# The fourth mixer of a two-block transformer kernel: TensorE's order written by hand, the index path first, two heads' queries at a time

## The chip, the cores and the metric

The kernel is one program on one core of a Trainium2 chip. A core has five engines that run side by side, each through its own queue of instructions: TensorE (PE in the profile: matmuls and transposes), VectorE (DVE), ScalarE (ACT), GpSimd (POOL) and SyncE (SP), which here issues the transfers. The metric is the time of one execution on the device in microseconds (us); less is better.

## The reference

Two transformer blocks run one after the other on 256 tokens of width 1024, all in 32-bit floats. The second block puts 16 meta tokens ahead of the 256 and has two layers: one with differential attention, one (the fourth mixer of the program) with an indexed latent attention, `_dsa_attention`. Each layer has two feed-forward networks around its mixer.

```python
def _dsa_attention(h, pos, cid, w_in, latent_norm, w_uq, q_norm, w_uv, rel_bias, k_sel):
    c_q, c_kv, k_idx, w_idx = jnp.split(h @ w_in, ...)        # 256, 256, 64 and 8 columns
    c_q = _rms_norm(c_q, latent_norm[0])
    c_kv = _rms_norm(c_kv, latent_norm[1])
    q_abs, q_idx = jnp.split(c_q @ w_uq, [B_HEADS * B_KV_RANK], axis=-1)   # 16 heads of 256; 8 index heads of 64
    q_abs = _rms_norm(q_abs.reshape(bsz, t, B_HEADS, B_KV_RANK), q_norm)
    k_idx = _rms_norm(k_idx)
    ...
        act = jax.nn.relu(jnp.einsum("bqhd,bsd->bqhs", qi, k_idx) * IDX_DIM ** -0.5)
        score = jnp.einsum("bqh,bqhs->bqs", wi, act)
        _, sel = lax.top_k(score, k_sel)                       # 64 keys of each query
        kv = gather(c_kv, sel)
        logits = jnp.einsum("bqhr,bqkr->bqhk", qa, kv) * B_KV_RANK ** -0.5 + bias
        p = jax.nn.softmax(jnp.where(valid, logits, NEG_INF), axis=-1)
        o_lat = jnp.einsum("bqhk,bqkr->bqhr", p, kv)
        o = jnp.einsum("bqhr,hrd->bqhd", o_lat, w_uv)
```

## The kernel before

**Precision.** A product of two 32-bit operands is made of three matmuls: each operand is split in a high and a low part, and `mm3` (L212 to L214) adds high·high, high·low and low·high. A weight arrives by DMA as `raw`, ScalarE casts its high part (`wh`, L187), and VectorE subtracts to get the low part (`wl`, L189). For the pieces in the table `ON_POOL` (L75) GpSimd does that subtraction. A piece has 1024 columns, or 512.

**Streaming.** `stream_plan` lists all weight pieces in the order of use, by name: `bw` (down-projection to the query latent), `bwi` (index key), `bw2` (key and value latent), `bwx` (index weights), `uqi` (index queries), `uq` (queries, two heads in a piece), `uv` (values, four heads in a piece). `take` hands out a piece; `ahead` starts the next loads, four pieces ahead.

**What sets the order.** Each engine runs its instructions in a fixed order that a tile scheduler chooses when the program is built, from the dependences and its own estimate of durations; the text of `dsa_mix` is only one input to it. A PSUM bank is a tile too: there are two tagged `mm`, two `s`, one `b`, one `n` and two `o`. A matmul that starts a new use of a bank stands behind the last read of its old use.

**The fourth mixer, `dsa_mix` (L991).** Rows are 272 tokens. From the normed input come the query latent (L1011 scales by the row's norm, L1023 and L225 split it into `cqh` and `cql`), the index key `ki` (L1036 to L1042), the key and value latent (L1047 to L1052: `ckg` for scores, `ckvh` and `ckvl` for values) and the index weights (L1060). Each of the 8 index heads has a score of all keys (matmuls L220), a relu on ScalarE (`rl`, L1084) and a weighted sum on VectorE (`sc`, L1089 for the first head, L1091 for the others; 16 instructions, since each head has two pieces of 272 and 144 columns). `top_rounds` then finds the 64 largest in eight rounds; a round is two MAX8 and two MATCH_REPLACE (L1104, L1105), all on VectorE and one behind another through `wk`. L1214 and L1215 make the mask `msk` of it.

Beside this, `prep(h)` projects one head's queries into an `mm` bank (12 matmuls), squares them on ScalarE (L1148), makes a norm of 128x2 numbers (`rsq`: Ln and Exp on ScalarE, L247 to L252; one refinement, on GpSimd for the first two heads, L255 to L257 with L258 on VectorE, on VectorE for the others, L261 to L263), scales the bank into `qx` (ScalarE at L1152 for heads 0 and 1, VectorE at L1154 for the others), transposes it into bank `n` (L1158) and copies it to `q` (L1160, ScalarE). The norm's result is `qst`.

`attend(h)` takes the scores of head h (L1177, bank `s`), adds bias and mask (L1179; GpSimd has added `msk` to the bias `nb` at L1165), takes the exponential (L1181), the reciprocal (L1183), scales (L1185, GpSimd), transposes the probabilities into bank `b` (`probs_t`, L977 to L980) and, for each two heads, multiplies by the values `v`, which `values(g)` makes for four heads at a time (18 matmuls, copies L1121 and L1124). Queries are made `LAG` = 4 heads ahead of `attend`.

Of the kernel before, what the change touches and what calls it, by code (L numbers as in the profile page):

```python
# [74 lines left out]
ON_POOL = {("uq", 0, 0), ("uq", 1, 0), ("bw2", 0, 0), ("bw2", 0, 1)}  # L75
# [4 lines left out]
def stream_plan():  # L80
# [32 lines left out]
    put("bwi", 1, 1024)  # L113
    put("bw2", 1, 2048)
    put("bwx", 1, 64)
# [5 lines left out]
    put("uq", 2, 1024, 3)  # L121
    put("uv", 1, 512, 2)
    put("uq", 2, 1024, 5)
    put("uv", 1, 512, 3)
    put("uq", 1, 1024, 7)
    wo(3)
    ffn(5)
    return plan


class Net:
    def __init__(self, ctx, tc, a, out):
# [75 lines left out]
    def mm3(self, out, w, x, first, last, chk=False):  # L208
        mm = self.nc.tensor.matmul
# [6 lines left out]
    def both(self, jobs, start, stop):  # L216


        for out, w, x in jobs[::-1]:
            self.nc.tensor.matmul(out, w, x, start=start, stop=stop, skip_group_check=True)  # L220
# [44 lines left out]
    def sumsq(self, src, cols, on_pool=()):  # L265
# [18 lines left out]
        if n > 1:  # L284
            nc.tensor.matmul(b[:, :cols], self.ones, acc[:, :cols], start=True, stop=False)
        nc.tensor.matmul(b[:, :cols], self.ones, sq[:, :cols], start=n == 1, stop=True)
# [204 lines left out]
    def cols_of(self, r_row, dst):  # L491

        b = self.bank("o")
        for tt in range(2):
            self.nc.tensor.transpose(b[:, tt * P : (tt + 1) * P], r_row[:, tt * P : (tt + 1) * P], self.ident)
        self.nc.vector.tensor_copy(dst, b[:, : 2 * P].rearrange("p (a b) -> p a b", a=2)[:, :, 0])

    def mem_pair(self, qm, mk, mv, p, y, pt, nb=2):
# [7 lines left out]
        for s in ss:  # L506
# [40 lines left out]
    def block1_mix0(self, Xr):  # L547
# [4 lines left out]
        with ExitStack() as ctx:  # L552
# [4 lines left out]
            for k in range(KD):  # L557
# [3 lines left out]
                nc.tensor.matmul(ss[:, :S], self.ones, sq, start=k == 0, stop=k == KD - 1)  # L561
# [55 lines left out]
    def block1_mix1(self, Xr):  # L617
        nc = self.nc
        self.banks(mm=2, z=4, o=2)
        with ExitStack() as ctx:  # L620
# [17 lines left out]
            def pair(p, q):  # L638
# [4 lines left out]
                for z in zs:  # L643
# [9 lines left out]
                    mm = nc.tensor.matmul  # L653
# [57 lines left out]
    def rel_table(self, pool):  # L711
# [9 lines left out]
        for lo, hi in ((0, 512), (512, RELW)):  # L721
            b = self.bank("o")
            nc.tensor.matmul(b[:16, : hi - lo], nrb, oh[:, lo:hi], start=True, stop=True)
# [22 lines left out]
    def boundary_ffn(self, X):  # L746

        nc = self.nc
        with ExitStack() as ctx:
# [19 lines left out]
            for b, sq, cols in zip(ss, sums, (S, T)):  # L769
                nc.tensor.matmul(b[:, :cols], self.ones, sq[:, :cols], start=True, stop=True)  # L770
# [14 lines left out]
    def diff_mix(self, X, Xf):  # L785
# [3 lines left out]
        with ExitStack() as ctx:  # L789
# [10 lines left out]
            nc.tensor.matmul(lb[:, :2], self.ones[:64], pr, start=True, stop=True)  # L800
# [27 lines left out]
            def prep(h):  # L828
# [16 lines left out]
                for i in range(2):  # L845
                    ss = self.bank("n")
                    nc.tensor.matmul(ss[:, :T], self.blk, sq[:, i], start=True, stop=True)  # L847
# [12 lines left out]
            def values(h):  # L860
# [7 lines left out]
                nc.tensor.transpose(b[:, 0], vx[:, 48 : 48 + P], self.ident)  # L868
                nc.tensor.transpose(b[:, 1], vx[:, 48 + P :], self.ident)
                nc.tensor.transpose(b[:48, 2], vx[:, :48], self.ident)  # L870
# [9 lines left out]
            def attend(h):  # L880
# [34 lines left out]
                for i, (oc, pc, v) in enumerate(self.v_parts(vr, vm[:, h], vq)):  # L915
                    nc.tensor.matmul(os[0][:, e * S + oc.start : e * S + oc.stop], v, pr[:, pc],  # L916
# [6 lines left out]
            def sub_norm(o, yh, yl, n, w, tag, tmp=(pt, "o", 2 * S)):  # L923
# [5 lines left out]
                nc.tensor.matmul(ss[:, :cols], self.ones, sq, start=True, stop=True)  # L929
# [4 lines left out]
            def meta(h0, h1):  # L934
# [14 lines left out]
                for h in range(n):  # L949
                    nc.tensor.transpose(b[:NM, h * NM : (h + 1) * NM], v[:, 0, h], self.ident[:NM, :NM])  # L950
# [3 lines left out]
                for h in range(n):  # L954
                    c = slice(h * NM, (h + 1) * NM)
                    nc.tensor.matmul(o[:, c], vm[:NM, h0 + h], ph[:, c], start=True, stop=True)
# [16 lines left out]
    def probs_t(self, L, pt, b, bufs=None):  # L973


        tr = self.nc.tensor.transpose
# [14 lines left out]
    def dsa_mix(self, X, Xr, Xf):  # L991
        nc, a = self.nc, self.a
        NH, LAG, NB = 16, 4, 3
        self.banks(mm=2, s=2, b=1, n=1, o=2)
        with ExitStack() as ctx:
            p1 = self.pool("dsas", 1, ctx=ctx)
            stage = ctx.enter_context(ExitStack())
# [31 lines left out]
            self.ahead()  # L1029
            xs, r = latent(bq, NM, S, pa)  # L1030
            for k in range(2):
                scaled(cq, k, 0, xs[k], self.g("cq", k), r, S)
            (bi,) = self.dense("bwi", xp, T, m_n=1)
            self.ahead()
# [4 lines left out]
            ssk = self.bank("n")  # L1039
            nc.tensor.matmul(ssk[:, :T], self.blk, kq, start=True, stop=True)  # L1040
            self.rsq(kq, ssk[:, :T], 64)
            nc.vector.scalar_tensor_tensor(ki, ki, 0.125, kq, ALU.mult, ALU.mult)  # L1042
            bk = self.dense("bw2", xp, T)
# [333 lines left out]
```

## Time and profile before

| | |
|---|---|
| median of 3 runs | 1721.84 us (1720.2 to 1722.18) |
| the profiled execution, its own time | 1716.95 us |
| span of its instructions | 1715.2 us |
| PE busy | 1678.1 us, 98% of the span |
| DVE busy | 1103.9 us, 64% |
| ACT busy | 895.9 us, 52% |
| POOL busy | 375.6 us, 22% |
| the fourth mixer, from the first `bwi` matmul to the start of its output projection | about 1380 to 1510 us of the span |

The profile comes from one execution. Every instruction has its start and duration on its engine; where an engine was idle, the trace says for how long and whose result ended it. The clock that the throttle granted to TensorE is given by stretch, 1.00 for the higher of its levels and 0.50 for half of that. All times of rows count from the start of the span; the execution's own time is 1.75 us longer than its span.

### The profile page before, as it was taken

Reading aid. Unit: us, or ns where it says so; the run is one execution under the profiler, and the core shown is the slowest. Engines: PE = TensorE matmul, PEld = TensorE weight load, DVE = VectorE, ACT = ScalarE, POOL = GpSimd, SP = SyncE. Lnnn points to the kernel's source line nnn. Section 1 sums busy time; section 2 is a strip of 40 time slices with the busy share of each in tenths; the row PEclk is TensorE's granted clock in tenths of the full one; section 3 lists DMA queues with packets and bytes.
Section 4 is the critical chain, followed back from the end, with each engine's and each line's share of the span. In section 5 each row is a group of like instructions: output and inputs, shape, how many; then the busy total and the mean of one; then the engine's idle time right before and its main releaser. Section 6 shows DMA issues by size and latency. Waiting matters only on the chain.

```text
span 1715.2 us, 32923 instructions
## 1 busy us (share of the span) xinstructions
PE 1678.1 (98%) x13474; PEld 1633.1 (95%) x13474; DVE 1103.9 (64%) x1808; ACT 895.9 (52%) x1554; POOL 375.6 (22%) x402
## 2 busy tenths in 40 slices
PE   7999999999999999999999999999999989999999
PEld 7999999998899999999988999999999977899999
DVE  7767666565766566655788766556665576666652
ACT  6545445476544555444566544445444457754441
POOL 3013220011322013211421222211221224432210
PEclk9999999999999999999999999999999999999999
DMA  8456655432555545445642454554454333335551
GB/s 282 167 195 225 229 185 185 172 124 99 174 195 179 191 172 174 177 176 180 193 127 89 147 174 174 174 182 171 177 177 174 124 126 126 124 136 186 183 192 69
DMA packets 59495, 287.56 MB, mean 168 GB/s; under 512 B 12064, under 2 KB 22816, under 8 KB 27472
## 3 DMA queue, kind: packets, MB, share of 16 engines
q1 hardware_dynamic: 58512, 284.80, 47.6%
q8 instruction: 106, 1.74, 0.4%
q10 hardware_dynamic: 832, 0.66, 0.1%
q14 instruction: 45, 0.37, 0.1%
HBM read 284.34 MB, written 5.53 MB: 169 GB/s over the span
## 4 chain that ended last, share of the span: by engine, by line
PE 92%; DVE 4%; ACT 1%; issue 1%; DMA 1%; POOL 0%; SPq 0%; ACTq 0%; DVEq 0%; POOLq 0%
PE mm L212 21%; PE mm L213 21%; PE mm L214 21%; PE z L214 8%; PE z L212 8%; PE z L213 8%; DVE wl L189 1%; PE s L1177 1%; PE o L220 1%; PE z L220 1%; DVE xl L229 1%; PE o L916 1%; DMA X<-in_xT_dram 1%; PE s L220 1%; PE n L847 0%
## 5 line engine op out<-in xcount | busy, mean ns | idle before, releaser
L187 ACT CAST wh<-raw 128x1024 fp32r<-128x1024 f32 (+1 forms) x521 | 540.5, 1040 | 634.3 <-PE mm L213 418.2
L189 DVE TENSOR_TENSOR wl<-raw,wh 128x1024 fp32r<-128x1024 f32 (+1 forms) x513 | 631.7, 1233 | 315.3 <-ACT wh L187 312.6
L212 PE MATMUL mm<-xh,wh 128*128 128x256 f32 (+2 forms) x1768 | 510.0, 289 | 5.4 <-DVE X L388 2.2
L213 PE MATMUL mm<-xl,wh 128*128 128x256 f32 (+2 forms) x1768 | 506.1, 286 | 4.0 <-DVE xl L229 3.7
L214 PE MATMUL mm<-xh,wl 128*128 128x256 f32 (+2 forms) x1768 | 506.3, 286 | 0.0
L212 PEld LDWEIGHTS mm<-xh,wh 128*128 128x128 f32 (+1 forms) x1768 | 333.4, 189 | 11.7 <-issue 2.8
L213 PEld LDWEIGHTS mm<-xl,wh 128*128 128x128 f32 (+1 forms) x1768 | 332.8, 188 | 8.0 <-DVE xl L229 4.9
L214 PEld LDWEIGHTS mm<-xh,wl 128*128 128x128 f32 (+1 forms) x1768 | 333.6, 189 | 1.2 <-issue 0.6
L214 PE MATMUL z<-xh,wl 128*128 128x256 f32 (+1 forms) x1088 | 311.0, 286 | 0.0
L213 PE MATMUL z<-xl,wh 128*128 128x256 f32 (+1 forms) x1088 | 309.9, 285 | 0.0
L212 PE MATMUL z<-xh,wh 128*128 128x256 f32 (+1 forms) x1088 | 309.6, 285 | 0.0
L212 PE MATMUL mm<-gh,wh 128*128 128x256 f32 (+1 forms) x1056 | 300.5, 285 | 0.0
L214 PE MATMUL mm<-gh,wl 128*128 128x256 f32 (+1 forms) x1056 | 299.5, 284 | 0.0
L213 PE MATMUL mm<-gl,wh 128*128 128x256 f32 (+1 forms) x1056 | 299.5, 284 | 0.0
L344 POOL TENSOR_TENSOR es<-es,r 128x256 f32<-128x256 f32 (+1 forms) x110 | 157.1, 1428 | 483.8 <-ACT es L343 483.8
L214 PEld LDWEIGHTS z<-xh,wl 128*128 128x128 f32 x1088 | 205.5, 189 | 0.2
L212 PEld LDWEIGHTS z<-xh,wh 128*128 128x128 f32 x1088 | 205.2, 189 | 0.0
L213 PEld LDWEIGHTS z<-xl,wh 128*128 128x128 f32 x1088 | 204.8, 188 | 0.0
L213 PEld LDWEIGHTS mm<-gl,wh 128*128 128x128 f32 x1056 | 199.2, 189 | 0.0
L214 PEld LDWEIGHTS mm<-gh,wl 128*128 128x128 f32 x1056 | 198.5, 188 | 0.0
L212 PEld LDWEIGHTS mm<-gh,wh 128*128 128x128 f32 x1056 | 198.4, 188 | 0.0
L345 DVE TENSOR_TENSOR ea<-z,es 128x256 f32<-128x256 f32 (+1 forms) x132 | 57.1, 433 | 96.1 <-PE z L214 52.1
(362 smaller groups left out, 1793.3 us busy)
## 6 DMA issues: line engine op xcount, KB each, us to landing
raw<-in_gu_dram SPq DMA_DIRECT2D x132, 1024.0 KB, 4.8
raw<-in_wd_dram SPq DMA_DIRECT2D x66, 1024.0 KB, 4.8
raw<-in_wo_dram SPq DMA_DIRECT2D x13, 1024.0 KB, 4.8
raw<-in_aw_dram SPq DMA_DIRECT2D x12, 1024.0 KB, 4.8
raw<-in_a_in_dram SPq DMA_DIRECT2D x9, 1024.0 KB, 5.3
nb<-scr SPq DMA_DIRECT2D x32, 136.0 KB, 2.4
scr<-relrow SPq DMA_DIRECT2D x16, 271.5 KB, 5.2
raw<-in_mkv_dram SPq DMA_DIRECT2D x4, 1024.0 KB, 4.8
```

The source lines that it names most:

```text
L187: self.nc.scalar.copy(h[:, :c], t[:, x : x + c])
L189: eng.tensor_tensor(l[:, :c], t[:, x : x + c], h[:, :c].bitcast(F32), ALU.subtract)
L212: mm(out, wh, xh, start=first, stop=False, skip_group_check=chk)
L213: mm(out, wh, xl, start=False, stop=False, skip_group_check=chk)
L214: mm(out, wl, xh, start=False, stop=last, skip_group_check=chk)
L220: self.nc.tensor.matmul(out, w, x, start=start, stop=stop, skip_group_check=True)
L229: self.nc.vector.scalar_tensor_tensor(l, src, col, h.bitcast(F32), ALU.mult, ALU.subtract)
L344: nc.gpsimd.tensor_tensor(s, s, r, ALU.mult)
L345: nc.vector.tensor_tensor(a, B[:, :cols], s, ALU.mult)
L916: nc.tensor.matmul(os[0][:, e * S + oc.start : e * S + oc.stop], v, pr[:, pc], start=e == 0 and i == 0, stop=e == 1 and i == 3, skip_group ...
L1177: nc.tensor.matmul(s[:, c], q[:, k, qc], ckg[:, k, k0 : k0 + n], start=k == 0, stop=k == 1)
```

## The change

The arithmetic of the reference and the matmuls that do it stay. What changes is the order, the banks and who does the small work of the fourth mixer:

- **Order by hand.** `Ordered` wraps TensorE's calls as `self.pe`. From `bwi` on until `turn(5)` has been written, every TensorE instruction of these lines is kept in the order of the text. Instructions of `attend` are written later and stay free for the scheduler.
- **Index first.** `bwi` goes to a bank `s`, `bwx` comes ahead of `bw2`, and the norm of the key and value latent moves from ahead of the index scores to between the rounds. `bw2`'s second half is cut in two around the third pair of index heads.
- **Two heads at a time.** `prep` becomes `project(h)`, which projects two heads into both `mm` banks and makes one norm of 128x4 numbers, on VectorE alone, and `turn(h)`, which transposes one head. ScalarE scales heads 0 to 5, VectorE the others. `LAG` becomes 6, and `values(1)` is written ahead of the last rounds.
- **Low parts on GpSimd.** `ON_POOL` gains `uq` pieces 2 and 3 and `uv` piece 0.

```diff
-ON_POOL = {("uq", 0, 0), ("uq", 1, 0), ("bw2", 0, 0), ("bw2", 0, 1)}
+ON_POOL = {("uq", j, 0) for j in range(4)} | {("bw2", 0, 0), ("bw2", 0, 1), ("uv", 0, 0)}
...
     put("bwi", 1, 1024)
+    put("bwx", 1, 64)
     put("bw2", 1, 2048)
-    put("bwx", 1, 64)
...
-        NH, LAG, NB = 16, 4, 3
+        NH, LAG, NB = 16, 6, 3
...
+            self.in_order = True
+            (bi,) = self.dense("bwi", xp, T, m_n=1, ps=("s",))
...
+            def project(h):
+
+                wq = self.take("uq", 2)
+                st = self.t(pq, [P, 2, 2], "qst")
+                b3s = []
+                for e in range(2):
+                    b3 = self.bank().rearrange("p (a b) -> p a b", a=2)
...
+                    qx = qxs[h + e] = self.t(pq, [P, 2, S], "qx")
+                    for tt in range(2):
+                        nc.scalar.activation(qx[:, tt], b3[:, tt], AF.Square, accum_out=st[:, e, tt : tt + 1])
+                    b3s.append(b3)
+                self.ahead()
+                v = st.rearrange("p a b -> p (a b)")
+                self.rsq(v, v, 256, tmp=(pq, "q", 4))
...
+            index_scores(0)
+            index_scores(2)
+            bk[1] = self.bank("n")
+            self.over_k(bk[1][:, :T], wk2[1], xks, range(KD), 0, 4)
+            index_scores(4)
+            self.over_k(bk[1][:, :T], wk2[1], xks, range(KD), 4, KD)
+            self.ahead()
+            index_scores(6)
...
+            project(0)
+            top_rounds(0, 1)
+            xs, r = latent(bk, 0, T, p1)
+            top_rounds(1, 2)
...
+            turn(0)
+            turn(1)
+            project(2)
             top_rounds(2, 4)
-            prep(2)
+            values(0)
+            turn(2)
+            turn(3)
+            project(4)
             top_rounds(4, 6)
-            prep(3)
-            values(0)
+            values(1)
+            turn(4)
+            turn(5)
+            self.in_order = False
             top_rounds(6, 8)
```

The orders below are those of the built programs: line, operation, result and operands, with a number for each tile. In the changed program all lines of the fourth mixer are 17 to 50 higher, and every TensorE instruction stands at L140.

**TensorE, first heads, before.** `s` are scores of a head, `mm_16634` a part of `values(0)` (its factors `ckvh`, `ckvl` and the `uv` weights), `b` the transposed probabilities of head 0, `n` the transposed queries of head 3.

```order
L1177 MATMUL s_16891<-ckg_16064,q_16573 128x144 x2
L1177 MATMUL s_16891<-ckg_16064,q_16573 128x272 x2
L212 MATMUL mm_16634<-wh_16316,ckvh_16062 128x256
L213 MATMUL mm_16634<-wl_16317,ckvh_16062 128x256
L214 MATMUL mm_16634<-wh_16316,ckvl_16063 128x256
L212 MATMUL mm_16634<-wh_16316,ckvh_16062 128x256
L213 MATMUL mm_16634<-wl_16317,ckvh_16062 128x256
L214 MATMUL mm_16634<-wh_16316,ckvl_16063 128x256
L977 MATMUL b_16737<-ident,L_2353_16438 128x128
L1158 MATMUL n_16619<-ident,qx_16606 128x128 x4
```

The same place after: scores of heads 0 and 1, the four transposes of head 0's probabilities, then `values(0)`.

```order
L140 MATMUL s_16827<-ckg_16067,q_16512 128x144 x2
L140 MATMUL s_16827<-ckg_16067,q_16512 128x272 x2
L140 MATMUL s_16860<-ckg_16067,q_16519 128x144 x2
L140 MATMUL s_16860<-ckg_16067,q_16519 128x272 x2
L140 MATMUL b_16839<-ident,L_2367_16492 128x128 x4
L140 MATMUL mm_16583<-wh_16314,ckvh_16065 128x256
L140 MATMUL mm_16583<-wl_16315,ckvh_16065 128x256
L140 MATMUL mm_16583<-wh_16314,ckvl_16066 128x256
```

Ahead of the first transposed probabilities stood three heads' scores, twelve matmuls of `values(0)` and the queries of heads 0 to 3, the first three of them transposed; now two heads' scores, no value, and the queries of heads 0 to 3, the first two of them transposed. `values(0)`, the turns of heads 2 and 3 and the third score stand behind.

**VectorE, from the first round to the first norm's result, before.** `m` are the eight largest, `qst_16456` is the norm of head 0, which the scaling at L1152 waits for.

```order
L1104 MAX m_2362_16477<-sc_16366 128x8
L1104 MAX m_2363_16480<-sc_16366 128x8
L1105 MATCH_REPLACE wk_16425<-m_2362_16477,sc_16366 128x272
L1105 MATCH_REPLACE wk_16425<-m_2363_16480,sc_16366 128x144
L1104 MAX m_2364_16483<-wk_16425 128x8
L1104 MAX m_2365_16486<-wk_16425 128x8
L1105 MATCH_REPLACE wk_16425<-m_2364_16483,wk_16425 128x272
L1105 MATCH_REPLACE wk_16425<-m_2365_16486,wk_16425 128x144
L258 SCALAR_TENSOR_TENSOR qst_16456<-qnr_16459,qnr_2359_16460 128x2
```

After, behind the second round: `qnr` and `qst_16407` are the norm of heads 0 and 1, `nr` and `latr` that of the key and value latent, `wl_16664` the low part of `uq` piece 5.

```order
L208 TENSOR_TENSOR wl_16664<-raw_16661,wh_16663 128x1024
L1121 MAX m_2383_16571<-wk_16267 128x8
L1121 MAX m_2384_16574<-wk_16267 128x8
L280 SCALAR_TENSOR_TENSOR qnr_2351_16447<-qst_16407,qnr_16446 128x4
L280 SCALAR_TENSOR_TENSOR nr_2364_16476<-o_16471,nr_16475 128x272
L1122 MATCH_REPLACE wk_16267<-m_2383_16571,wk_16267 128x272
L1122 MATCH_REPLACE wk_16267<-m_2384_16574,wk_16267 128x144
L281 SCALAR_TENSOR_TENSOR qnr_2351_16447<-qnr_2351_16447,qnr_16446 128x4
L281 SCALAR_TENSOR_TENSOR nr_2364_16476<-nr_2364_16476,nr_16475 128x272
L1121 MAX m_2385_16577<-wk_16267 128x8
L1121 MAX m_2386_16580<-wk_16267 128x8
L282 SCALAR_TENSOR_TENSOR qst_16407<-qnr_2351_16447,qnr_16446 128x4
```

The norm's result came behind two rounds; it comes behind two rounds, a low part, a third round and the two MAX of a fourth, with two steps of the latent's norm between.

**GpSimd, the same stretch, before.** `wl_16250` and `wl_16256` are the low parts of `uq` pieces 0 and 1.

```order
L189 TENSOR_TENSOR wl_16250<-raw_16247,wh_16249 128x1024
L189 TENSOR_TENSOR wl_16256<-raw_16253,wh_16255 128x1024
L1047 TENSOR_TENSOR lat_2307_16259<-lat_2307_16259,latr_2314_16270 128x272
L1047 TENSOR_TENSOR lat_2309_16261<-lat_2309_16261,latr_2314_16270 128x272
L1052 COPY ckvh_16062<-ckvh_16062 128x2x32
```

After, with `uv` piece 0 (`wl_16315`) and `uq` pieces 2 and 3 (`wl_16321`, `wl_16557`):

```order
L208 TENSOR_TENSOR wl_16218<-raw_16215,wh_16217 128x1024
L208 TENSOR_TENSOR wl_16309<-raw_16264,wh_16308 128x1024
L208 TENSOR_TENSOR wl_16315<-raw_16312,wh_16314 128x512
L208 TENSOR_TENSOR wl_16321<-raw_16318,wh_16320 128x1024
L208 TENSOR_TENSOR wl_16557<-raw_16554,wh_16556 128x1024
L1244 MEMSET L_2367_16492 128x16
L1244 MEMSET L_2368_16493 128x16
L1246 TENSOR_TENSOR lat_2355_16463<-lat_2355_16463,latr_2362_16474 128x272
```

Three subtractions come ahead of the scaling of the key and value latent, and that scaling itself has moved behind the first rounds.

## Rows read from the trace of the kernel before

**Rows 1.** The page: busy time, share of the span and instructions of each engine
```profile
PE 1678.1 (98%) x13474; PEld 1633.1 (95%) x13474; DVE 1103.9 (64%) x1808; ACT 895.9 (52%) x1554; POOL 375.6 (22%) x402
```

**Rows 2.** 2-us stretches: length, busy PE, PEld, DVE, ACT, POOL, clock, DMA share, GB/s
```profile
1404.00:1406.00 2.00, 0.94 (x9) 0.57 (x5) 2.00 (x6) 1.41 (x4) 0.11 (x1) 1.00 0.88 270
1406.00:1408.00 2.00, 0.00 (x0) 0.00 (x0) 2.00 (x8) 2.00 (x9) 0.00 (x0) 1.00 0.63 183
1408.00:1410.00 2.00, 0.00 (x0) 0.00 (x0) 2.00 (x10) 0.72 (x5) 0.59 (x3) 0.55 0.51 131
1410.00:1412.00 2.00, 1.00 (x5) 0.82 (x5) 2.00 (x12) 1.30 (x5) 0.16 (x1) 0.50 0.00 0
1412.00:1414.00 2.00, 2.00 (x12) 2.00 (x11) 2.00 (x13) 1.22 (x3) 0.43 (x3) 0.50 0.00 0
1414.00:1416.00 2.00, 2.00 (x11) 1.89 (x11) 2.00 (x10) 1.25 (x6) 0.00 (x0) 0.74 0.00 0
```

**Rows 3.** PE in order of time: start, duration, line, result, [idle before, whose result ended it]
```profile
1396.94 0.49 PE L220 MATMUL s<-ki,qi 64*128 64x272 f32 x1
...
1411.00 1.27 PE L1158 MATMUL n<-ident,qx 128*128 128x128 f32 x4 [6.06 <-ACT qx L1152]
...
1421.88 1.67 PE L1177 MATMUL s<-ckg,q 128*128 128x144 f32 x8 [0.97 <-ACT q L1160]
...
1425.38 0.33 PE L977 MATMUL b<-ident,L 128*128 128x128 f32 x1 [1.12 <-POOL L L1185]
...
1427.51 0.27 PE L979 MATMUL b<-ident,L 128*128 128x128 f32 x1
1427.62 0.27 PE L980 MATMUL b<-ident,L 128*128 128x128 f32 x1
...
1429.13 1.57 PE L1177 MATMUL s<-ckg,q 128*128 128x144 f32 x8
1430.33 0.48 PE L212 MATMUL mm<-wh,ckvh 128*128 128x256 f32 x1
1430.65 0.28 PE L213 MATMUL mm<-wl,ckvh 128*128 128x256 f32 x1
1430.77 0.28 PE L214 MATMUL mm<-wh,ckvl 128*128 128x256 f32 x1
...
1432.30 0.39 PE L212 MATMUL mm<-wh,ckvh 128*128 128x256 f32 x1 [0.45 <-ACT v L1121]
```

**Rows 4.** DVE in order of time, as rows 3
```profile
1398.51 0.91 DVE L1089 TENSOR_SCALAR sc<-rl,wc 128x272 f32<-128x272 f32 x1 [0.89 <-ACT rl L1084]
...
1400.78 1.21 DVE L189 TENSOR_TENSOR wl<-raw,wh 128x1024 fp32r<-128x1024 f32 x1
...
1407.80 0.66 DVE L1104 MAX8 m<-sc 128x8 f32<-128x272 f32 x2
...
1419.51 0.37 DVE L1215 TENSOR_SCALAR msk<-msk 128x432 f32<-128x432 f32 x1
...
1421.58 1.84 DVE L189 TENSOR_TENSOR wl<-raw,wh 128x1024 fp32r<-128x1024 f32 x1
```

**Rows 5.** POOL in order of time, as rows 3
```profile
1365.47 2.40 POOL L189 TENSOR_TENSOR wl<-raw,wh 128x1024 fp32r<-128x1024 f32 x1 [4.07 <-ACT wh L187]
...
1397.77 1.49 POOL L1047 TENSOR_TENSOR lat<-lat,latr 128x272 f32<-128x272 f32 x2 [12.40 <-DVE latr L263]
...
1419.96 4.98 POOL L1165 TENSOR_TENSOR nb<-nb,msk 128x144 f32<-128x144 f32 x7 [7.37 <-DVE msk L1215]
```

**Rows 6.** Line L229: count, least/median/greatest duration in ns, first and last start
```profile
L229 DVE SCALAR_TENSOR_TENSOR xl<-X,gains,xh x2: 495/1232/1970, 1366.2 to 1375.6; 128x272 fp32r<-128x272 f32 x2
L229 DVE SCALAR_TENSOR_TENSOR ckvl<-lat,gains,ckvh x2: 486/486/486, 1401.9 to 1402.3; 128x272 fp32r<-128x272 f32 x2
```

**Rows 7.** The same columns as rows 2: nine stretches of 8 us, 1438 to 1510, summed
```profile
sum 72.00, PE 70.37 PEld 62.32 DVE 46.09 ACT 52.90 POOL 26.01; mean PE 7.82 PEld 6.92 DVE 5.12 ACT 5.88 POOL 2.89
```

**Rows 8.** A short idle time of PE near 1522, as rows 3
```profile
1523.33 0.39 PE L213 MATMUL mm<-xl,wh 128*128 128x256 f32 x1 [1.91 <-DVE xl L229]
```

**Rows 9.** The same columns as rows 2: two stretches around rows 8
```profile
1522.00:1524.00 2.00, 0.67 (x5) 0.67 (x6) 2.00 (x4) 0.35 (x1) 1.79 (x2) 1.00 0.38 70
1524.00:1526.00 2.00, 2.00 (x11) 1.81 (x10) 2.00 (x4) 0.47 (x2) 0.00 (x0) 0.57 0.89 360
```

More of the change, by code (lines that the diff above doesn't have):

```diff
@@ L219, in both @@
         for out, w, x in jobs[::-1]:
-            self.nc.tensor.matmul(out, w, x, start=start, stop=stop, skip_group_check=True)
+            self.pe.matmul(out, w, x, start=start, stop=stop, skip_group_check=True)
     def split_act(self, h, l, src):
@@ L722, in rel_table @@
             b = self.bank("o")
-            nc.tensor.matmul(b[:16, : hi - lo], nrb, oh[:, lo:hi], start=True, stop=True)
+            self.pe.matmul(b[:16, : hi - lo], nrb, oh[:, lo:hi], start=True, stop=True)
             nc.vector.tensor_copy(t[:, lo:hi], b[:16, : hi - lo])
@@ L769, in boundary_ffn @@
             for b, sq, cols in zip(ss, sums, (S, T)):
-                nc.tensor.matmul(b[:, :cols], self.ones, sq[:, :cols], start=True, stop=True)
+                self.pe.matmul(b[:, :cols], self.ones, sq[:, :cols], start=True, stop=True)
             r1 = self.t(p, [P, S], "r1")
@@ L799, in diff_mix @@
             lb = self.bank("n")
-            nc.tensor.matmul(lb[:, :2], self.ones[:64], pr, start=True, stop=True)
+            self.pe.matmul(lb[:, :2], self.ones[:64], pr, start=True, stop=True)
             le = p1.tile([P, 2], F32, name="lame")
@@ L928, in sub_norm @@
                 ss = self.bank(tag)
-                nc.tensor.matmul(ss[:, :cols], self.ones, sq, start=True, stop=True)
+                self.pe.matmul(ss[:, :cols], self.ones, sq, start=True, stop=True)
                 self.rsq(sq, ss[:, :cols], P, tmp=tmp)
@@ L1038, in dsa_mix @@
             nc.scalar.activation(kq, ki, AF.Square)
[L1039 to L1043, printed above, removed]
-            self.ahead()
-            xs, r = latent(bk, 0, T, p1)
-            for k in range(2):
-                nc.gpsimd.tensor_tensor(xs[k], xs[k], r, ALU.mult)
-                nc.vector.tensor_scalar(ckg[:, k, P:], xs[k], gk[:, k : k + 1], None, ALU.mult)
-                self.split_scaled(ckv[0][:, k, 32:], ckv[1][:, k, 32:], xs[k], self.g("ckv", k))
-            nc.scalar.copy(ckg[:, :, :P], ckg[:, :, P + NM : P + NM + P])
-            for i in range(2):
-                nc.gpsimd.tensor_copy(ckv[i][:, :, :32], ckv[i][:, :, 32:64])
             w = self.take("bwx", KD)
@@ L1155, in prep, with turn @@
+            def turn(h):
+                qx = qxs.pop(h)
                 bt = self.bank("n").rearrange("p (a b) -> p a b", a=2)
```

144 lines of the change are left out of this document (81 added, 63 removed).

## Prediction

> **What bounds the kernel now.** I read the page first. TensorE is busy for 1678.1 of 1715.2 us [rows 1], so outside the fourth mixer there is little to win, and TensorE's order outside it is unchanged. Inside I read TensorE's 2-us stretches: it does nothing from 1404.7 to 1411.0, and its clock then stands at half, the lower of its two levels (1.2 of 2.4 GHz), until about 1415 [rows 2]. TensorE in order of time names what ended each wait: 6.06 us until the scaled queries of head 0 at 1411.00, 0.97 us until a copy of queries, 1.12 us until the first probabilities at 1425.38, 0.45 us until a copy of values [rows 3]. Last I read who made those late. VectorE is the answer: busy for every instant of 1404 to 1414 [rows 2], with the weighted sums from 1398.51, the rounds from 1407.80 and the mask ready at 1419.51 + 0.37 = 1419.88 [rows 4]. So two things wait for VectorE's serial work: the first queries (only a small norm, which stands among the rounds) and the mask, behind which lies GpSimd's bias, idle for 7.37 us until then [rows 5]. The reader is to see that the second is the harder bound: nothing of `attend` can be finished before the mask, and TensorE has only a fixed stock of other work to fill that time.
>
> **The change, part by part.**
>
> *Index path.* Ahead of the first index scores, half of `bw2` is gone (24 matmuls, about 0.12 us apart by the pitch of rows 3, so 3 us) and one more group of index queries has come (six, 0.7 us). From 1396.94 [rows 3] that gives 1394.6; the queries now wait some 0.6 us for `cqh`/`cql` and the first copy, since less work stands between. I take 1395.2. In before, 1.57 us passed from scores to the first weighted sum (1396.94 to 1398.51), so 1396.8 is possible.
>
> *Low parts on GpSimd.* GpSimd takes 2.40 us for a piece [rows 5] and VectorE 1.21 [rows 4]. What matters is whom they stop. The subtraction of `X` at L229 took 1970 ns when it began at 1366.2, under GpSimd's low part of 1365.47 to 1367.87, and 486 to 495 ns otherwise [rows 5, 6]; it ended when GpSimd was through. L1089, 0.91 us long at 1398.51, lay under GpSimd's 1.49 us from 1397.77 [rows 4, 5]. In the changed order the cast of `uq` piece 3 stands on ScalarE right at the last index queries, so GpSimd's subtraction runs from about 1396.3 to 1398.7. The first weighted sum then starts at 1398.9 and not at 1396.8: the head start of the index path is eaten. Bounds: 0 (1396.8) and 2.1 us; I take 2.1, as the L229 row is the nearest to it. The page "SBUF — State Buffer" of the Trainium skill, section "Who interferes with whom", says that a VectorE instruction with two SBUF inputs and a GpSimd instruction that reads SBUF exclude each other for the whole instruction; the trace agrees (1970 against 495 ns), and the rule speaks against this edit. By it the sum is the one below; without it the first rival's.
>
> *VectorE from the first sum to the mask.* Before, 1419.88 - 1398.51 = 21.4 us without a gap worth naming. Gone from this stretch: a low part of 1024 (1.1), one of 512 (0.6, now behind the mask), two scalings of queries (0.9) and small norms (0.4). New in it: low parts of `uq` pieces 4 and 5 (2.3), three steps of the latent's norm at about 0.45 (1.35) and three steps of 128x4 at 0.1 (0.3). Net +0.9: 22.3. The mask is then ready at 1398.9 + 22.3 = 1421.2, 1.3 us later than before. The bounds come from the start alone: 1419.1 to 1421.2.
>
> *The first idle time.* The norm of heads 0 and 1 stands behind two rounds, a low part, a third round and half a fourth. That is some 13.5 us behind the first sum, where it was 11.8, so the first transposes start at about 1413, not 1411.00. This lengthens the 6.06 us by some 1.5, but I count it at nothing: from 1413 TensorE still does, partly at half clock, two turns, 24 projections and two scores, which end near 1422, and then it waits for the mask anyway. If that cover is gone (a mask before 1417), it costs up to 2.
>
> *What stands behind the mask.* From the mask to the first transposed probabilities 1425.38 - 1419.88 = 5.5 us passed [rows 3, 4], with a VectorE low part of 1.84 us in it [rows 4]. Behind the mask VectorE now has a low part of 512 and the norm of heads 2 and 3, and both reciprocals stand behind both heads' bias. Bounds 4.4 and 5.5; I take 5.5, the only row for it. The first probabilities are transposed from 1421.2 + 5.5 = 1426.7 and done, with four at 0.11 [rows 3], at 1427.1. Before, they were done at 1427.62 + 0.11 = 1427.7. But now `values(0)`, two turns and a head's scores stand behind them: 18 matmuls at 0.117 (2.1), eight transposes at 0.11 (0.9) and 1.4 for scores (1429.13 to 1430.65, one matmul between [rows 3]), together 4.4 us that TensorE had done before. At equal work: 1427.1 + 4.4 = 1431.5 against 1427.7, **+3.8 us**. TensorE's order being fixed, it cannot take the values during the wait, though their inputs are there by then.
>
> *Later waits.* In each new pair two scores stand together and then the first one's transposes. Between score and transposes lie bias, exponential, reciprocal and scaling: the 5.5 us less 0.6 for GpSimd's first bias and 1.84 for the low part, some 3.1. The second head's scores cover 1.4 of it, so the third head's transposes wait about 1.7. The turns of heads 3 and 6 wait for the copy out of the single bank `n`, or for a norm that holds both `mm` banks: 0.7 and 0.6; `values(1)` 0.6. That is 3.6. Before's own later waits go: 0.45 at 1432.30 [rows 3], and of the 72.00 - 70.37 = 1.6 us between 1438 and 1510 [rows 7] about half, so -1.3. Net **+2.3 us**; bounds -2.1 (all of before's go, none comes) and +3.6. With six heads ahead and half as many norms (8 for 16) I see no steady wait after the fourth pair, and there is only that 1.6 to win.
>
> *Other edits.* Both banks and the wrapper cost nothing by themselves; the 128x4 norm is as long as a 128x2 within 0.1 us and is hidden by matmuls once queries are six heads ahead. If that cover goes, each pair pays about 0.6.
>
> Sum: 3.8 + 2.3 = **+6.1 us**. The profiled execution, 1716.95, would become 1723.1. It lies 4.9 below the median of the runs, 1721.84, and I move the median by the same: 1727.9.
>
> **The rivals.**
>
> *Same: GpSimd's low parts stop nobody.* The mask is ready at 1419.1, and the chain behind it takes 4.4, since no long low part of VectorE meets it: transposes done at 1423.9, equal work at 1428.3, +0.6. With the later waits +2.9, so 1724.7. For it speaks that ScalarE may place the cast a little later or earlier than I think; against it, the L229 and L1089 rows. It decides if the first weighted sum starts before 1397.5.
>
> *Faster: the index path's head start reaches the mask.* If the mask is ready by 1417, the first probabilities stand at 1421.4 and nothing of TensorE waits for it: equal work at 1421.4 + 0.4 + 4.4 = 1426.2, -1.5. With it all of before's later waits go, -2.1, so -3.6 and 1718.2. For it: 6.06 us of idle time are there to be had, and the edits aim at them. Against it: VectorE's work up to the mask is not less, and it would have to start 3.6 us earlier than in before's 21.4 us plus 0.9, at 1394.7, before its scores.
>
> *Slower still: the clock falls a second time.* Between the second head's scores (1422) and the probabilities (1426.7) TensorE stands for over 4 us. A wait of 1.91 us [rows 8] was followed by a stretch at 0.57 [rows 9]; some 4 us at that clock lose 1.7. If the waits for held banks come back at five of the later pairs, 0.6 each, that is 3.0 more: +10.8, 1732.6. It decides if the granted clock near 1427 is below 0.7.
>
> **How the numbers follow.** Forecast 0.50; GpSimd stops nobody 0.24; faster 0.13; slower still 0.13. The likeliest is 1727.9. About 0.2%, 3.4 us, is what a measurement of this kernel can tell from no change, so faster means under 1718.4. The forecast's own bounds are 1723.5 (later waits at -2.1) and 1729.2 (at +3.6). The range reaches down past the same-time rival, with its chain at the low end and part of before's waits gone, to 1720.5, which leaves out the faster case, and up to 1732: 0.13 and some 0.06 stand outside. Faster 0.13, same 0.24, slower 0.63.
>
> **What would show it.** Right: the first L1089 (now 18 lines lower) starts near 1399 and directly behind a GpSimd low part; MAX8 of round 5 or later still runs when the first turn starts; the mask ends near 1421; TensorE has a wait of about 4 us that ends with GpSimd's scaling ahead of `b`, with `values(0)` right behind it; and the stretch from the first `bwi` to the output projection is some 6 us longer. Wrong: a first sum before 1397.5, no VectorE instruction lengthened under GpSimd's low parts, a mask before 1419, or a wait ahead of `b` under 2 us. If the mixer is longer but by waits elsewhere (the `mm` banks held by a norm), the sum is right by accident, and the step on the mask is the one that fell.

## The result and the profile after

| | before | after |
|---|---|---|
| median | 1721.02 us (4 runs) | 1733.16 us (4 runs, 1731.96 to 1734.41) |
| ratio to before, 95% interval | | 1.0071, 1.0053 to 1.0088 |
| profiled execution, its span | 1716.95, 1715.2 | 1731.96, 1730.2 |
| first `bwi` matmul to the end of the span | 1380.11 to 1715.2: 335.1 us | 1382.78 to 1730.2: 347.4 us |

The changed kernel is slower by 12.1 us. Its profile is 15.0 us longer, but 2.7 of these lie ahead of the mixer, where TensorE's order is the same (1.7 of them are a wait near 44 us that took 2.43 and takes 4.14). The profiles of the experiments below start the mixer at 1382 us or later too (e4, whose order is that of before but for a few matmuls, at 1383.56), so those 2.7 belong to the one execution of before. From `bwi` on it is 12.3 us.

The stretch of 175 us that holds the mixer, from both traces (columns as in [rows 2]), first before, then after:

```profile
1370.00:1545.00 175.00, 162.38 (x1263) 147.86 (x1262) 122.12 (x332) 115.31 (x312) 62.84 (x94) 0.97 0.39 129
```

```profile
1370.00:1545.00 175.00, 152.94 (x1160) 138.44 (x1159) 98.48 (x283) 109.11 (x290) 66.48 (x90) 0.94 0.34 110
```

TensorE stands for 22.1 us instead of 12.6. Besides, the clock is at its lower level more often: busy time times (1 - granted clock), summed over 1-us stretches, is 7.4 us instead of 3.7. That is 9.5 and 3.7 more, together 13 us: the whole loss is TensorE waiting, and the clock falling behind its waits. No other engine is near full in the stretch (ScalarE is the busiest, 109 of 175 us).

TensorE of after in order of time, the answer to [rows 3]:

```profile
1382.78 0.29 PE L140 MATMUL s<-xh,wh 128*128 128x272 f32 x1
...
1414.93 1.26 PE L140 MATMUL n<-ident,qx 128*128 128x128 f32 x4 [6.62 <-ACT qx L1172]
1416.90 1.11 PE L140 MATMUL n<-ident,qx 128*128 128x128 f32 x4 [0.71 <-ACT q L1184]
...
1421.99 2.98 PE L140 MATMUL s<-ckg,q 128*128 128x144 f32 x16
1427.72 1.50 PE L140 MATMUL b<-ident,L 128*128 128x128 f32 x4 [2.76 <-POOL L L1209]
1428.87 0.56 PE L140 MATMUL mm<-wh,ckvh 128*128 128x256 f32 x1
...
1435.17 0.66 PE L140 MATMUL n<-ident,qx 128*128 128x128 f32 x4 [0.84 <-ACT q L1184]
...
1444.22 0.33 PE L140 MATMUL b<-ident,L 128*128 128x128 f32 x1 [2.77 <-POOL L L1209]
...
1490.03 0.63 PE L140 MATMUL b<-ident,L 128*128 128x128 f32 x4 [1.08 <-ACT qnr L271]
...
1500.81 0.30 PE L140 MATMUL n<-ident,qx 128*128 128x128 f32 x1 [1.49 <-DVE qx L1174]
```

The wait of [rows 3] ahead of the first turn is still there (6.62 for 6.06). New are two waits of 2.8 us ahead of `b`, and waits of over 1 us as late as 1500, where [rows 7] had 1.6 us in 72. The two waits are each followed, as the first one is, by a stretch at the lower clock:

```profile
1428.00:1430.00 2.00, 1.88 (x9) 1.69 (x9) 0.00 (x0) 1.67 (x5) 1.76 (x5) 0.50 0.57 148
1430.00:1432.00 2.00, 2.00 (x15) 2.00 (x14) 0.00 (x0) 0.76 (x3) 1.87 (x3) 0.74 0.00 0
...
1446.00:1448.00 2.00, 2.00 (x11) 2.00 (x11) 0.00 (x0) 0.71 (x2) 0.46 (x1) 0.50 0.58 201
```

VectorE of after, the answer to [rows 4]: the low part of the query latent, the first two weighted sums, the end of the mask, and the first step of the norm of heads 2 and 3. Below it, ScalarE's scaling of heads 2 and 3 and of heads 4 and 5.

```profile
1391.31 2.63 DVE L244 TENSOR_TENSOR cql<-ea,cqh 128x256 fp32r<-128x256 f32 x2
...
1399.26 2.13 DVE L1107 TENSOR_SCALAR sc<-rl,wc 128x272 f32<-128x272 f32 x2 [2.77 <-ACT rl L1102]
...
1422.62 0.39 DVE L1268 TENSOR_SCALAR msk<-msk 128x432 f32<-128x432 f32 x1
...
1425.36 0.57 DVE L280 SCALAR_TENSOR_TENSOR qnr<-qst,qnr 128x4 f32<-128x4 f32 x1
```

```profile
1427.55 1.54 ACT L1172 ACTIVATE qx<-mm,qst 128x256 f32<-128x256 f32 x4
...
1443.24 1.54 ACT L1172 ACTIVATE qx<-mm,qst 128x256 f32<-128x256 f32 x4
```

From the first `bwi` matmul the mask took 1423.01 - 1382.78 = 40.2 us, 39.8 before. The norm and the scaling were the key later: the projections of heads 2 and 3 ended at about 1422.2, and their two `mm` banks were read for the last time at about 1428.3 and 1429.1 (two of the four instructions of 1427.55 for each bank). `values(0)` writes to `mm` banks. Behind these projections it could not have started before 1428.3; it started at 1428.87. In the next pair the banks were read until about 1444.0 and 1444.8, and `values(1)` started at 1445.37.

Not all of the second wait is the banks'. GpSimd's scaling of head 2's probabilities, which ended it, had its reciprocal at 1442.73 but began at 1443.74, behind an addition to a later head's bias `nb` that waited for its transfer:

```profile
1443.29 0.49 POOL L1189 TENSOR_TENSOR nb<-nb,msk 128x144 f32<-128x144 f32 x1 [11.42 <-DMA nb<-scr]
1443.74 1.02 POOL L1209 TENSOR_TENSOR L<-L,ast 128x144 f32<-128x144 f32 x2
```

That is about 1.0 of the 2.77 us.

### The profile page after: what moved, and what is told of

Its sections match the earlier page's. It is cut to its first block, busy times and chain, and to the rows that moved or that the text cites. A ratio compares the mean times of both kernels' runs of the same rounds, so it can differ in the third digit from the quotient of the medians.

```text
span 1730.2 us, 32862 instructions
## 1 busy us (share of the span) xinstructions
PE 1684.2 (97%) x13474; PEld 1638.5 (95%) x13474; DVE 1091.3 (63%) x1777; ACT 897.9 (52%) x1544; POOL 379.1 (22%) x399
## 4 chain that ended last, share of the span: by engine, by line
PE 90%; DVE 4%; ACT 3%; DMA 1%; issue 1%; POOL 0%; SPq 0%; ACTq 0%; DVEq 0%; POOLq 0%
PE mm L140 61%; PE z L140 24%; PE o L140 2%; PE s L140 1%; PE n L140 1%; DVE wl L208 1%; ACT wh L206 1%; DVE xl L248 1%; DMA X<-in_xT_dram 1%; DVE X L407 0%; PE t L140 0%; DMA raw<-in_a_in_dram 0%; PE b L140 0%; POOL sqa L300 0%; ACT qx L1162 0%
## 5 line engine op out<-in xcount | busy, mean ns | idle before, releaser
L208 DVE TENSOR_TENSOR wl<-raw,wh 128x1024 fp32r<-128x1024 f32 (+2 forms) x510 | 626.8, 1230 | 330.2 <-ACT wh L206 327.6
L140 PE MATMUL mm<-xh,wh 128*128 128x256 f32 (+2 forms) x1744 | 502.9, 289 | 8.0 <-DVE X L407 5.0
L140 PE MATMUL mm<-xl,wh 128*128 128x256 f32 (+2 forms) x1744 | 499.2, 286 | 2.1 <-DVE xl L248 1.8
L140 PE MATMUL mm<-xh,wl 128*128 128x256 f32 (+2 forms) x1744 | 499.2, 286 | 0.0
L140 PEld LDWEIGHTS mm<-xh,wh 128*128 128x128 f32 (+1 forms) x1744 | 329.3, 189 | 13.9 <-ACT xh L247 3.0
L140 PEld LDWEIGHTS mm<-xl,wh 128*128 128x128 f32 (+1 forms) x1744 | 328.5, 188 | 5.7 <-DVE xl L248 2.6
L140 PEld LDWEIGHTS mm<-xh,wl 128*128 128x128 f32 (+1 forms) x1744 | 329.2, 189 | 1.1 <-issue 0.6
L140 PE MATMUL z<-xh,wl 128*128 128x256 f32 (+1 forms) x1088 | 310.8, 286 | 0.0
L140 PE MATMUL z<-xl,wh 128*128 128x256 f32 (+1 forms) x1088 | 310.2, 285 | 0.0
L140 PE MATMUL z<-xh,wh 128*128 128x256 f32 (+1 forms) x1088 | 309.9, 285 | 0.0
L140 PE MATMUL mm<-gh,wh 128*128 128x256 f32 (+1 forms) x1056 | 300.5, 285 | 0.0
L140 PE MATMUL mm<-gh,wl 128*128 128x256 f32 (+1 forms) x1056 | 299.5, 284 | 0.0
L140 PE MATMUL mm<-gl,wh 128*128 128x256 f32 (+1 forms) x1056 | 299.5, 284 | 0.0
L140 PEld LDWEIGHTS z<-xh,wl 128*128 128x128 f32 x1088 | 205.8, 189 | 0.1
L140 PEld LDWEIGHTS z<-xh,wh 128*128 128x128 f32 x1088 | 205.5, 189 | 0.0
L140 PEld LDWEIGHTS z<-xl,wh 128*128 128x128 f32 x1088 | 205.1, 188 | 0.0
L140 PEld LDWEIGHTS mm<-gl,wh 128*128 128x128 f32 x1056 | 199.2, 189 | 0.0
L140 PEld LDWEIGHTS mm<-gh,wl 128*128 128x128 f32 x1056 | 198.6, 188 | 0.0
L140 PEld LDWEIGHTS mm<-gh,wh 128*128 128x128 f32 x1056 | 198.3, 188 | 0.0
```

The lines of the kernel that those rows point to most:

```text
L140: ins = f(*args, **kw)
L208: eng.tensor_tensor(l[:, :c], t[:, x : x + c], h[:, :c].bitcast(F32), ALU.subtract)
```

## The experiments

All times are medians beside runs of the kernel before (1720.4 to 1721.5 us in these comparisons); the ratio is to those.

| kernel | us | ratio to before (95%) |
|---|---|---|
| after | 1733.16 | 1.0071 (1.0053 to 1.0088) |
| e1, after with the old low parts | 1732.82 | 1.0063 (1.0048 to 1.0078) |
| e2, after without hand order | 1733.78 | 1.0070 (1.0055 to 1.0085) |
| e4, before with the new low parts | 1720.55 | 0.9996 (0.9987 to 1.0006) |
| e5, after, hand order carried on | 1756.95 | 1.0207 (1.0188 to 1.0227) |
| e6, after, a norm for each head | 1721.24 | 1.0007 (0.9997 to 1.0016) |
| e7, after, four heads ahead | 1736.40 | 1.0091 (1.0076 to 1.0107) |
| e8, before with two-head norms | 1737.86 | 1.0100 (1.0085 to 1.0115) |
| e9, before with the index path first | 1723.48 | 1.0014 (1.0004 to 1.0024) |
| e10, after, values in banks `o` | 1728.40 | 1.0040 (1.0025 to 1.0054) |
| e11, after, banks copied out | 1730.98 | 1.0056 (1.0041 to 1.0071) |
| e12, before, six heads ahead | 1718.19 | 0.9984 (0.9975 to 0.9993) |
| e13, after, three `mm` banks | 1717.47 | 0.9981 (0.9972 to 0.9991) |
| e14, before, three `mm` banks | 1716.45 | 0.9973 (0.9963 to 0.9982) |
| e15, e12 with three `mm` banks | 1716.47 | 0.9975 (0.9965 to 0.9984) |

### First theories: the fixed order (A) and GpSimd's low parts (B)

**e1**, only the table back:

```diff
-ON_POOL = {("uq", j, 0) for j in range(4)} | {("bw2", 0, 0), ("bw2", 0, 1), ("uv", 0, 0)}
+ON_POOL = {("uq", 0, 0), ("uq", 1, 0), ("bw2", 0, 0), ("bw2", 0, 1)}
```

> The changed kernel with only the table of GpSimd's low parts put back, so VectorE makes those of queries 2 and 3 and of values 0; TensorE's order in the mixer is the same row for row. Theory A (TensorE's fixed order costs most: the first probabilities' transposes stand ahead of the values, turns and projections, and the same again for the second pair): 1730 to 1732 us, at most 3 under the changed kernel's 1733, and the waits ahead of b of heads 0 and 2 stay over 2 us. Theory B (GpSimd's low parts, which stop VectorE for 1.5 to 2.6 us at a time, cost most): 1722 to 1725 us and a mask about 2 us earlier.

1732.82 us. B falls as the cause of the time. Its mechanism doesn't: the two rows of VectorE that lay under GpSimd's low parts are short again.

```profile
1394.38 0.74 DVE L244 TENSOR_TENSOR cql<-ea,cqh 128x256 fp32r<-128x256 f32 x2
...
1400.43 0.56 DVE L1107 TENSOR_SCALAR sc<-rl,wc 128x272 f32<-128x272 f32 x2
```

0.74 for 2.63 and 0.56 for 2.13. In this trace the mask is ready 38.4 us after the first `bwi` matmul (1423.08 - 1384.68), 1.8 earlier than in after. The first probabilities come 1.8 us earlier with it (43.1 us behind `bwi` for 44.9), and TensorE waits for them no less than in after:

```profile
1427.81 1.50 PE L140 MATMUL b<-ident,L 128*128 128x128 f32 x4 [3.16 <-POOL L L1209]
```

Of these 1.8 us 0.6 are left at the next pair's scores: the clock stands at its lower level until about 1433.7, nearly 6 us behind the wait where in after it was 3.3 (over the 175 us the lower level costs 8.5 us, in after 7.4). The kernel is 0.3 us faster by the medians and 1.4 by the ratios, which these runs can't tell from nothing. So the mask sets when the first `b` can run, but **its lateness is not what the 12 us are made of**.

**e4**, the new table in the kernel before:

> The kernel before with only the new table of GpSimd's low parts; TensorE's order is its own but for a few matmuls of one group. Theory A: 1720 to 1724 us, the cost of stopped VectorE instructions alone. Theory B: 1728 us or more.

1720.55 us, no change beyond the interval. Either way round, the low parts cost or bring nothing that these runs can tell.

**e2**, the order free:

```diff
-            self.in_order = True
```

> The changed kernel with TensorE's order left to the scheduler everywhere; everything else of the change stays, GpSimd's low parts too. The scheduler then puts two thirds of the values and a turn ahead of the first probabilities. Theory A: 1723 to 1727 us, since the wait ahead of b of head 0 is filled and the later ones too. Theory B: 1731 to 1734 us.

1733.78 us. A falls too. The scheduler does put twelve matmuls of the values ahead of the first `b`, but they stand behind the scaling that frees their banks, and TensorE now waits ahead of them and in other places:

```profile
1426.16 0.33 PE L140 MATMUL n<-ident,qx 128*128 128x128 f32 x1 [2.51 <-ACT qx L1171]
...
1455.91 0.85 PE L140 MATMUL n<-ident,qx 128*128 128x128 f32 x4 [2.72 <-DVE qx L1173]
...
1501.35 0.33 PE L140 MATMUL b<-ident,L 128*128 128x128 f32 x1 [2.71 <-POOL L L1208]
```

Where in after a wait stood ahead of `b`, one stands ahead of the queries' transposes, nearly as long. In the 175 us from 1370 TensorE stands for 22.5 us, in after 22.1. The order moved the wait and did not fill it.

**e5**, the order carried on by hand (attend is split into scores and the rest):

```diff
-            turn(4)
-            turn(5)
-            self.in_order = False
...
+            for h in range(0, NH, 2):
+                scores(h)
+                scores(h + 1)
...
+                if h % 4 == 0:
+                    values(h // 4)
+                if h + 2 < NH:
+                    turn(h + 2)
+                    turn(h + 3)
...
+                if h + 4 < NH:
+                    project(h + 4)
...
+                    attend(h + e)
+                if h == 10:
+                    self.in_order = False
```

> The changed kernel with the hand order carried on through the heads: for each pair scores, then values, the turns of the next pair and the projection of the one after, and only then the transposes of the pair's probabilities; free from the sixth pair's end. Theory A: the waits ahead of b go (nothing over 1 us behind the first turn until the last pairs), 1718 to 1723 us. Theory B: 1728 us or more, since the mask is as late as in the changed kernel.

This edit also makes queries only four heads ahead. 1756.95 us, 36 slower than before. My order put two uses of a single bank side by side, two turns into `n` and two heads' transposes into `b`:

```profile
1444.58 0.63 PE L140 MATMUL b<-ident,L 128*128 128x128 f32 x4 [2.06 <-ACT pr L1001]
1445.88 1.31 PE L140 MATMUL o<-pr,v 128*64 128x256 f32 x16 [0.68 <-ACT pr L1001]
...
1451.92 0.66 PE L140 MATMUL n<-ident,qx 128*128 128x128 f32 x4 [1.29 <-ACT q L1184]
```

Each pair waits some 4 us for ScalarE to copy those banks out. So this run decides nothing between A and B, though its time lies where B was expected; it points at banks.

### Which part of the change: two-head norms (C), six heads ahead (D), index path (E)

**e6**, the norm inside the loop over the two heads:

```diff
-                st = self.t(pq, [P, 2, 2], "qst")
...
                 for e in range(2):
+                    st = self.t(pq, [P, 2], "qst")
...
-                    b3s.append(b3)
-                self.ahead()
-                v = st.rearrange("p a b -> p (a b)")
-                self.rsq(v, v, 256, tmp=(pq, "q", 4))
-                for e, b3 in enumerate(b3s):
...
+                    self.rsq(st, st, 256, tmp=(pq, "q", 2))
...
+                self.ahead()
```

> The changed kernel with a norm of its own for each head again (still projected two at a time, hand order kept): each head's bank is scaled and freed as soon as its own squares are there. Theory C (one norm for two heads holds both mm banks and makes turns and transposes late): 1722 to 1727 us. Theory D (six heads ahead, with ScalarE scaling six of them) and theory E (the index path first, with the latent's norm among the rounds): still 1731 to 1734.

1721.24 us: the loss is gone but for 0.9 us, within the interval, with hand order, index path, low parts and six heads as in after. In its trace two groups of values stand ahead of the first `b`, and only one of them waits:

```profile
1424.86 0.48 PE L140 MATMUL mm<-wh,ckvh 128*128 128x256 f32 x1
...
1427.90 0.39 PE L140 MATMUL mm<-wh,ckvh 128*128 128x256 f32 x1 [1.98 <-ACT qx L1166]
```

The first uses the bank of head 2, which was scaled at 1424.5; the second waits for head 3's scaling.

**e8**, the reverse, two-head norms put into the kernel before (`prep` replaced by `project` and `turn`):

> The kernel before with only the two-head projection and its one norm on VectorE; index path, four heads ahead, free order and low parts are its own. Theory C: 1728 to 1734 us, most of the loss by this part alone. Theory D and E: 1720 to 1723.

1737.86 us, above the range of C. This part alone costs 17 us; its edit also takes the first heads' refinement from GpSimd and projects heads 1 and 3 a step earlier. **e7**, `LAG` 4 in after:

> The changed kernel with queries four heads ahead again and the old order of the weight pieces behind it; two heads' norms, index path and low parts stay. Theory D: 1722 to 1727. Theory C and E: 1731 to 1735, or more, since the two-head norms have less lead.

1736.40 us: six heads ahead do not cost, they save 3 us. That they do so as a lead that hides part of the loss is likely but not shown. **e9**, the index path alone in the kernel before:

> The kernel before with only the index path first: bwi in a bank s, bwx ahead of bw2, the latent's norm among the rounds; heads one by one, four ahead, free order, old low parts. Theory E: 1728 to 1734. Theory C and D: 1719 to 1723.

1723.48 us, some 2.5 us slower (0.7 to 4.1 by the interval; between what C and E expected, and a small part). So C holds: taking the two-head norm out of after gives back 11 to 12 us, and putting it into before costs 17. The parts do not add up one by one.

### How the two-head norm costs: held banks (C1) or late queries (C2)

**e10**: `b = self.bank("o")` in `values`.

> The changed kernel with only the values' matmuls in the banks o instead of mm, so that they need not wait until a two-head norm gives the mm banks back. Theory C1 (the held mm banks are the cost of the two-head norm): 1723 to 1728 us, values of heads 0 to 3 ahead of the first probabilities. Theory C2 (it is the lateness of the queries themselves): 1730 to 1734, the turns and the projections wait as before.

1728.40 us, 4.8 of the 12.1 back: just above the range of C1 and below that of C2. The trace suggests why it is no more. The values do run early, twelve of their matmuls from 1422.18, but the order on ScalarE changed as well: the scaling of heads 2 and 3 stands ahead of the first head's exponential, and the first probabilities come 47.6 us behind `bwi` (1430.48 - 1382.90) instead of 44.9.

```profile
1426.55 1.57 ACT L1172 ACTIVATE qx<-mm,qst 128x256 f32<-128x256 f32 x4 [1.93 <-DVE qst L282]
1427.99 0.43 ACT L1205 ACTIVATE L<-L,ast 128x144 f32<-128x144 f32 x1
```

```profile
1430.48 0.33 PE L140 MATMUL b<-ident,L 128*128 128x128 f32 x1 [2.49 <-POOL L L1209]
```

**e11**, the banks copied out behind the squares and scaled in place:

```diff
                         nc.scalar.activation(qx[:, tt], b3[:, tt], AF.Square, accum_out=st[:, e, tt : tt + 1])
-                    b3s.append(b3)
+                    nc.scalar.copy(qx, b3)
+                    b3s.append(qx)
```

> The changed kernel with both heads' projections copied out of their mm banks by ScalarE right behind the squares and scaled in place later; the norm is still one for two heads and as late. Costs ScalarE one 512-column copy a head, about 0.6 us each. Theory C1: 1720 to 1727. Theory C2: 1731 or more.

1730.98 us, at the edge of C2's range. The values now follow the scores without a wait, but other long waits end with ScalarE, which has the copies to do (two of them):

```profile
1432.70 0.63 PE L140 MATMUL b<-ident,L 128*128 128x128 f32 x4 [2.91 <-ACT pr L1001]
...
1471.68 0.66 PE L140 MATMUL n<-ident,qx 128*128 128x128 f32 x4 [2.39 <-ACT q L1185]
```

That the copies are what costs here is argued from these rows, not shown, so e11 doesn't tell C1 from C2. **e13** does, one `mm` bank more and no work more:

```diff
-        self.banks(mm=2, s=2, b=1, n=1, o=2)
+        self.banks(mm=3, s=2, b=1, n=1, o=1)
```

> The changed kernel with a third bank mm in the fourth mixer, taken from the two banks o. A two-head norm then holds two of three. Theory C1 (held mm banks): 1720 to 1726 us, the values ahead of the first probabilities and waits ahead of b under 1.5 us. Theory C2 (late queries): 1730 to 1735.

1717.47 us, 15.7 under after. A group of values runs ahead of the scores and another behind them, and the wait ahead of `b` is half. The two-head norm is nearly as late as it was: from the first `bwi` matmul (1382.43), the first turn starts 0.5 us later than in after and the scaling of heads 2 and 3 1.1 earlier.

```profile
1421.87 0.28 PE L140 MATMUL mm<-wh,ckvh 128*128 128x256 f32 x1
...
1427.69 0.33 PE L140 MATMUL b<-ident,L 128*128 128x128 f32 x1 [1.43 <-POOL L L1209]
```

Over the same 175 us TensorE stands for 12.7 us, as in before, and the lower clock costs 2.3 us instead of 7.4:

```profile
1370.00:1545.00 175.00, 162.28 (x1287) 149.62 (x1286) 110.82 (x300) 117.00 (x304) 71.69 (x93) 0.98 0.40 127
```

**e14**, the same line in the kernel before:

> The kernel before with the same three banks mm and one bank o. One norm for each head holds one bank at a time, so the third should be worth little: theory C1 and C2 both 1718 to 1723 us, unless the lost bank o makes the pairs' outputs wait, then up to 1727.

1716.45 us, 4.5 under before and below what I expected: a bank is worth something there too. Beside it, after with three banks is 1.0 us slower instead of 12.1 (each of the two ratios is known to some 0.001, 1.7 us). So about 11 of the 12 us are there only while there are two `mm` banks: C1. What stays open is why e10 and e11, which free the banks in other ways, gave back only 5 and 2 us; that ScalarE's new order or new work took the rest is read from their waits, not tested.

**e12**, the kernel before with `LAG` 6, `prep(4)`, `prep(5)` and `values(1)` ahead of the last rounds:

> The kernel before with only the queries made six heads ahead instead of four (two heads more ahead of the mask, the second group of values too, the weight pieces in that order); one norm for each head, its own index path, free order and low parts. If the two heads more fill TensorE's wait for the mask, as they gave 3 us inside the changed kernel: 1716 to 1719 us, faster than both kernels. If VectorE and ScalarE, which must norm and scale them, only get later: 1720 to 1724.

1718.19 us, 2.8 under before by the ratio. **e15**, both:

> The kernel before with queries six heads ahead and three banks mm, one o. If the bank adds to the six heads' gain: 1714 to 1717 us. If not: 1717 to 1720; if the lost bank o costs: 1720 to 1725.

1716.47 us, as e14: the six heads add nothing to the third bank. The intervals of e12 to e15 all lie below before. The shortest way there is e14, one line in the kernel before; e13, e14 and e15 can't be told from each other.

## Why the prediction had the sign right and the size and the cause wrong

**The sign was right, the size was half.** +6.1 us were forecast and +12.1 came; 1733.16 lies above the range's 1732.0. The terms, from the first `bwi` matmul on:

| step | predicted | measured |
|---|---|---|
| first index scores | 15.1 us | 14.7 |
| first weighted sum through | about 19.7 | 18.4 |
| first turn later than before by | 1.5 to 2 | 1.3 |
| mask | 41.1 | 40.2 |
| mask to first probabilities | 5.5 (4.4 to 5.5) | 4.7 |
| loss at equal work | +3.8 | +4.9 |
| later waits | +2.3 (-2.1 to +3.6) | +7.4 |

For equal work, turn 3 of after ended at 1435.58; less `b` of head 1 (0.44) and the first output (1.24), which before had not done by then, plus the third score (1.42), 52.5 us against 47.6. The rest of 12.3 is 7.4.

**The step that failed** is the price of the held banks. It stood in the term for later waits, +2.3 with +3.6 as its upper bound, half of the 7.4 that came. I had found that a norm holds both `mm` banks, priced it together with the copy out of `n` at 0.7 and 0.6 us for two turns, and wrote of the norm that it "is hidden by matmuls once queries are six heads ahead". It was not hidden: both banks were held from 1422 to 1428 and again in the next pair (behind waits of 2.76 and 2.77). By e6, and by e13 beside e14, it makes 11 to 12 us, so it is behind the loss at equal work as well; e8 puts even more on the two-head norm.

**A right number with a wrong cause.** The 4.4 us of work that stands behind the first probabilities were there, but the sentence that TensorE "cannot take the values during the wait, though their inputs are there by then", because its order was fixed, fell with e2: free order, same time. The operands were there; the bank to write was not, and with a third bank (e13) a group of values ran at 1421.87. That this term came close, 3.8 for 4.9, is luck. I had looked at inputs and order and not at what the result needs. In that place the order was a consequence: with one norm for each head the scheduler put the values first by itself, under the same hand order (e6).

**The mask as the bound** fell with e1, as an account of the loss: the mask 1.8 us earlier brought the first probabilities 1.8 us earlier, and 0.4 was left from `bwi` to the end of the span. The prediction had said what this would mean: a mixer that is longer by waits for held `mm` banks makes its sum right by accident.

**Low parts.** That GpSimd's low parts stop VectorE was right where it was read (2.63 and 2.13 us, 0.74 and 0.56 without). The Trainium skill's rule in "SBUF — State Buffer", section "Who interferes with whom", agrees with the first of these rows, a subtraction with two operands in SBUF; the second has only one tensor operand there, and the rule on two does not cover it. What the low parts slowed did not show in the time, which moved by 0.3 us in e1 and by 0.6 in e4, both within the intervals.

**The rivals.** "Slower still" came nearest, 1732.6, and its signs are in the trace: the clock is at 0.50 from 1427.7, where it set its mark, and waits came back in later pairs. Its price for the banks, 0.6 a pair, was right only in sum with my other terms. The rival of the same time needed low parts that stop nobody, and they did stop VectorE. The faster one needed a mask by 1417; it came at 1423.01, or 1420.3 in the times of before.

**The signs.** The marks were given in the times of before, whose mixer starts 2.7 us earlier. Moved by that, the first weighted sum started at 1396.6, which is the same-time rival's mark (before 1397.5) and not the forecast's (near 1399), though its ground was wrong: the sum took 1.94 us under GpSimd's low part, and half of the head start was lost in it. The mask was ready at 1420.3, and the wait ahead of `b` was 2.76 us where about 4 were expected.

**Slips in the working** that change nothing: TensorE does nothing from 1404.9 (1411.00 - 6.06), not 1404.7, and in the faster rival 1394.7 lies 3.8 us ahead of 1398.51, not 3.6.

## What to carry to other kernels

Before two results are joined to halve a small operation, count how long each holds its PSUM bank, and who else writes to that tag: joining makes the first result wait for the second, and the whole norm and both scalings lie between two uses of the bank. Ask of every instruction that might fill a wait not only whether its inputs are there but where it writes. One bank moved from a tag that is seldom used to the one that is held (e14, 4.5 us in one line) was worth more than the best reordering tried here (e12, 2.8 us), though their intervals overlap.

## What the runs showed of the hardware

While GpSimd subtracted 128x1024 numbers in SBUF (1390.74 to 1393.31 and 1398.62 to 1401.00), a VectorE instruction with its tensors in SBUF ended only behind it: two of 128x256 took 2.63 us together and 0.74 without it, two of 128x272 and 128x144 took 2.13 and 0.56. One that reads a PSUM bank (L1067, at 1390.98) was not held up, 0.41 against 0.40 in e1. TensorE's granted clock fell to the lower level, 0.50, behind waits of 2.76 and 2.77 us, and stayed there for about 3 us of work each time; behind the wait of 3.16 us in e1 it stayed for nearly 6. Over the stretch of the mixer the lower level cost 7.4 us in after and 3.7 in before. I had expected one fall of the clock behind the mask, in a rival.
